# Forgetting attention's value projection, written tile by tile between the first thirteen slots with TensorE's order pinned

## The chip, the cores and the metric

One core of one Trainium2 chip runs the whole program. The metric is the device time of one execution, in microseconds (us). Engines are called PE (TensorE's matmuls), PEld (its weight loads), DVE (VectorE), ACT (ScalarE), POOL (GpSimd) and SP (SyncE, which here issues the transfers). Line numbers (L188) are those of the kernel before, where nothing else is said.

## The reference, cut to what matters

The reference is one decoder layer on 1024 tokens of width 1024. The first block has two groups of heads side by side on the same normalized input: four mLSTM heads of width 128 and eight heads of forgetting attention of width 64. A cross-attention and an MLP follow.

```python
h = rmsnorm(x, ln1[l])
z = h @ w_in[l]
ml_qk, ml_v, ml_o, ml_i, ml_f, fx_q, fx_k, fx_v, fx_f = jnp.split(z, splits, axis=-1)
...
mh = mlstm_chunkwise(mq, mk, mv, ig, lf)
...
fv = fx_v.reshape(B, S, FX_HEADS, FX_DH)
flf = jax.nn.log_sigmoid(fx_f.astype(jnp.float32) + fx_b_f[l].astype(jnp.float32))
fx_out = forgetting_attention(fq, fk, fv, flf).reshape(B, S, FX_W)
x = x + jnp.concatenate([ml_out, fx_out], axis=-1) @ w_out[l]
```

In `forgetting_attention` the scores of a block of 128 queries get a decay per key, are masked, go through a softmax, and weigh the values `fv`. The change is about where `fx_v`, a product of `h` (1024 x 1024) with 512 columns of weights, is computed in time.

## The kernel before

Every float32 operand of a large product is kept as a pair, high and low part (`split`, L131 to L138: ACT copies the high part, DVE forms the remainder), and a product is three matmuls (`mm3`, L183 to L188). The normalized input `h` lies in SBUF as pairs, features on partitions.

The order of the work is set in two ways. The program is traced in the order in which it is written, and a scheduler, which simulates the engines, then puts each engine's instructions in an order of its own: an instruction that is written later may stand earlier if it is ready earlier in that simulation. Where the code says `with in_order(...)` (L144), the instructions written inside are chained: on each named engine they keep their written order, behind the last instruction that was chained on it. Once built, each engine's order is fixed, and an engine waits at an instruction until its operands and its buffer are there.

Around the change stand these pieces:

- `ml_head(hd, ...)` (L568) is one mLSTM head, a generator in four steps. The first step goes over two halves of the tokens and four blocks of 128 keys in each: a score on PE into a bank of PSUM called "sc"; a decay on ACT (L586) with a mask on POOL (L588); their product on DVE (L589); its split on ACT and DVE (L134, L135); a sum over blocks on POOL (L593); and the product with the values on PE into the bank "ov". Sums over the 128 partitions (L217), a reciprocal root (L198 to L208, the power on POOL in L204) and the factors `fac` (L617) end the step. The next step turns the factors into a row (`to_row`: a transpose on PE in L249, a copy on ACT in L250, a transfer to DRAM in L251 and back to all partitions in L253). The third multiplies the first half's output with that row and the gate (L628, L629), splits and stores it, and loads the second half's row (L625). The fourth does the same for the second half. These three later steps are `closing`, and `next(closing, None)` runs one of them.
- "sc" has three banks that are used in turn, "tp" two, "mm", "m2" and "ov" one each. The last head's eight scores, its two groups of sums, the slots' scores and the row's transpose take the three "sc" banks in the order in which they are written.
- `slot(values, until)` (L1026) is a step of forgetting attention, one part of a score (up to 512 keys of 128 queries) after the other: the maximum of the part before on DVE (`top`, L741, L744), the exponential of the one before that on ACT (`exp`, L756), a scaling on POOL (L767), and the two matmuls of a new part's score (L734, L735). It is all under `in_order`. The first thirteen slots (`LEAD_`) run without values; from the fourteenth on, the probabilities are transposed (L782) and multiplied with the values (L801).
- `token_major(w_src, sink, cs, between)` (L488) is a projection with tokens on partitions. For each of two groups `c` of 256 columns it loads and splits two weight tiles (`weights`: "wr" has two buffers, "wh" and "wl" three each), and for each of eight blocks `t` of 128 tokens it runs 24 matmuls of 128x256 into a bank ("mm", "tp", "m2", "tp" in turn) and then `sink`. A tile in the text is one such block of 24 matmuls, numbered 0 to 15. Their three uses of "wh" and "wl" mean that group 1's second weight tile (k from 4 on) takes the buffer of group 0's first one, which is free when half of tile 7's matmuls are done.
- `fv_sink` (L649) splits the result (L137, L138) and stores it to DRAM (L652), from where a head's values are loaded later (L849).

Before, the thirteen slots are written first, then the projection as a whole. None of its instructions is under `in_order`, so the scheduler lays them wherever the engines have room.

## Time and profile before

| what | us |
|---|---|
| timed runs, median of 3 (lowest to highest) | 1511.64 (1510.98 to 1512.29) |
| span of the profiled execution | 1509.2 |
| timed median less that span (no other time of the profiled execution is given) | 2.4 |
| PE, sum of its busy time | 1493.0 |
| last mLSTM head's first key scores end, first value tile's matmul starts | 331.1 |
| slot 0's score on PE | 351.0 |
| first transpose of probabilities on PE (slot 13) | 392.8 |

A row of a timeline has the start in us, the length in us (of a group, where xN is over 1), the engine, the line, the operation, the tile written and those read, and, in brackets, how long the engine stood idle before it and what ended that. Matmuls overlap: one of 128x512 shows 0.39 us, but follows the one before after about 0.23 us. A row of busy times by stretches has the stretch, its length, each engine's busy time with the number of its instructions, the granted TensorE clock (1.00 is full speed), the share of the transfer engines and GB/s.

### The profile page before, as it was taken

The numbers are of one execution on the slowest core, as the hardware profiler recorded it, in microseconds if no ns is written. First come the engines' busy times: TensorE is split into PE (matmuls) and PEld (weight loads), VectorE is DVE, ScalarE is ACT, GpSimd is POOL, SyncE is SP. The second block draws the span as 40 slices with busy tenths as digits, with TensorE's granted clock in tenths as the row PEclk, the third lists the DMA queues.
The fourth block names the chain that finished last, engine by engine and source line by source line (L and its number), as shares of the span: only waits on it lengthen the run. The fifth ranks groups of instructions, "written<-read, shape, count | busy, mean of one in ns | idle before, by whom it ended". The sixth has DMA issues, their size and how long they took to land.

```text
span 1509.2 us, 22358 instructions
## 1 busy us (share of the span) xinstructions
PE 1493.0 (99%) x7806; PEld 1263.7 (84%) x7806; DVE 1122.7 (74%) x1803; ACT 757.7 (50%) x1440; POOL 528.7 (35%) x545
## 2 busy tenths in 40 slices
PE   9999999999999999999999999999999999999997
PEld 9988888889899888788988878888888888888887
DVE  7766676664788875667767899989996678787765
ACT  7324343334688764566654467566664521122134
POOL 1003030414365441623300044454544365553312
PEclk9999999999999999999999999999999999999999
DMA  6322333435777877853354447676678677776623
GB/s 243 115 79 95 98 108 126 132 129 153 247 261 256 284 248 246 271 169 126 128 182 159 147 155 279 235 261 248 217 273 292 264 279 279 279 272 251 247 88 112
DMA packets 124276, 303.04 MB, mean 201 GB/s; under 512 B 13810, under 2 KB 28460, under 8 KB 117252
## 3 DMA queue, kind: packets, MB, share of 16 engines
q1 hardware_dynamic: 124164, 301.62, 57.3%
q8 instruction: 61, 1.00, 0.3%
q14 instruction: 51, 0.42, 0.1%
HBM read 202.75 MB, written 98.82 MB: 200 GB/s over the span
## 4 chain that ended last, share of the span: by engine, by line
PE 90%; DMA 4%; DVE 3%; ACT 1%; issue 1%; POOL 1%; POOLq 0%; DVEq 0%; SPq 0%; ACTq 0%
PE tp L186 8%; PE tp L187 8%; PE tp L188 8%; PE sc L186 6%; PE sc L188 6%; PE sc L187 6%; PE mm L186 5%; PE m L188 5%; PE m L186 5%; PE m L187 5%; PE mm L188 5%; PE mm L187 5%; PE ov L801 2%; PE ov L186 2%; PE ov L187 2%; PE ov L188 2%
## 5 line engine op out<-in xcount | busy, mean ns | idle before, releaser
L186 PE MATMUL tp<-act,wl 128*128 128x512 f32 (+1 forms) x440 | 172.6, 392 | 0.0
L187 PE MATMUL tp<-act,wh 128*128 128x512 f32 (+1 forms) x440 | 172.1, 391 | 0.0
L188 PE MATMUL tp<-act,wh 128*128 128x512 f32 (+1 forms) x440 | 171.8, 392 | 0.0
L135 DVE TENSOR_TENSOR wl<-wr,wh 128x1024 fp32r<-128x1024 f32 (+2 forms) x99 | 131.4, 1327 | 27.0 <-ACT wh L134 26.7
L134 ACT ACTIVATE wh<-wr 128x1024 fp32r<-128x1024 f32 (+2 forms) x99 | 99.8, 1008 | 85.7 <-PE tp L188 32.7
L186 PE MATMUL mm<-act,wl 128*128 128x512 f32 (+1 forms) x332 | 124.8, 376 | 2.6 <-DVE r_c L138 2.1
L188 PE MATMUL mm<-act,wh 128*128 128x512 f32 (+1 forms) x332 | 124.1, 374 | 0.0
L187 PE MATMUL mm<-act,wh 128*128 128x512 f32 (+1 forms) x332 | 123.8, 373 | 0.0
L186 PE MATMUL m<-act,wl 128*128 128x512 f32 (+1 forms) x308 | 113.8, 369 | 0.6 <-DVE wl L135 0.6
L188 PE MATMUL m<-act,wh 128*128 128x512 f32 (+1 forms) x308 | 113.8, 369 | 0.0
L187 PE MATMUL m<-act,wh 128*128 128x512 f32 (+1 forms) x308 | 113.7, 369 | 0.0
L188 PE MATMUL sc<-act,wh 128*128 128x512 f32 (+1 forms) x280 | 105.6, 377 | 0.0
L187 PE MATMUL sc<-act,wh 128*128 128x512 f32 (+1 forms) x280 | 105.6, 377 | 0.0
L186 PE MATMUL sc<-act,wl 128*128 128x512 f32 (+1 forms) x280 | 105.6, 377 | 0.0
L1612 POOL TENSOR_TENSOR z<-wr 128x256 f32<-128x256 f32 x56 | 52.9, 966 | 131.8 <-DMA wr<-w_ff2q 126.7
L188 PEld LDWEIGHTS tp<-act,wh 128*128 128x128 f32 x440 | 82.7, 188 | 19.0
L186 PEld LDWEIGHTS tp<-act,wl 128*128 128x128 f32 x440 | 82.7, 188 | 18.5
L187 PEld LDWEIGHTS tp<-act,wh 128*128 128x128 f32 x440 | 82.7, 188 | 18.2
L134 ACT ACTIVATE wh<-z 128x1024 fp32r<-128x1024 f32 (+1 forms) x54 | 55.5, 1027 | 81.8 <-POOL z L1612 62.3
L135 DVE TENSOR_TENSOR wl<-z,wh 128x1024 fp32r<-128x1024 f32 (+1 forms) x54 | 77.7, 1439 | 11.4 <-ACT wh L134 11.4
L134 ACT ACTIVATE w<-wr 128x768 fp32r<-128x768 f32 (+3 forms) x35 | 28.0, 801 | 107.4 <-PE tp L186 33.0
L186 PEld LDWEIGHTS mm<-act,wl 128*128 128x128 f32 x332 | 62.7, 189 | 14.2 <-DVE r_c L138 2.6
(734 smaller groups left out, 4387.2 us busy)
## 6 DMA issues: line engine op xcount, KB each, us to landing
act<-right SPq DMA_DIRECT2D x49, 1024.0 KB
right<-w SPq DMA_DIRECT2D x56, 256.0 KB
wr<-w_ff2q SPq DMA_DIRECT2D x28, 512.0 KB
right<-r_d SPq DMA_DIRECT2D x49, 256.0 KB
right<-r_e SPq DMA_DIRECT2D x49, 256.0 KB
act<-fqk SPq DMA_DIRECT2D x48, 256.0 KB
wr<-w_in SPq DMA_DIRECT2D x20, 512.0 KB
wr<-w_ff SPq DMA_DIRECT2D x20, 512.0 KB
```

The source lines that it names most:

```text
L134: s.activation(hi, src, AF.Copy)
L135: return v.tensor_tensor(out=lo, in0=src, in1=hi.bitcast(F32), op=ALU.subtract)
L186: nc.tensor.matmul(ps, w[1], x[0], start=first, stop=False, skip_group_check=more)
L187: nc.tensor.matmul(ps, w[0], x[1], start=False, stop=False, skip_group_check=more)
L188: nc.tensor.matmul(ps, w[0], x[0], start=False, stop=last, skip_group_check=more)
L801: nc.tensor.matmul(self.ov[:, c0:], self.fv[:, self.j], t[:, c0:], start=self.j == 0 and t is self.p[1], stop=self.last and t is self.p[0])
L1612: g.tensor_tensor(out=o, in0=x, in1=y, op=op)
```

## The change

`token_major` yields after every tile, and its caller drives it. The projection's sixteen tiles are now written between the slots: two behind each of slots 0, 1 and 2 and one behind each of slots 3 to 12, and on PE (on PE alone) they are chained with the slots' matmuls. The steps of `closing` are now all written inside the loop: behind slots 1, 6 and 11, where before they stood behind slots 1 and 11 and ahead of the projection's tile 4.

```diff
                 sink(t, c, ps)
+                yield
...
-    token_major(a["w_mv"], mv_sink, (1,), {2: row_first, 4: gate_rows})
+    for _ in token_major(a["w_mv"], mv_sink, (1,), {2: row_first, 4: gate_rows}):
+        pass
...
+    fv_tiles = token_major(a["w_fv"], fv_sink)
     for i in range(LEAD_):
         slot(False, 0)
-        if i in (1, 11):
+        if i in (1, 6, 11):
             next(closing, None)
-    token_major(a["w_fv"], fv_sink, between={4: lambda: next(closing, None)})
+        with in_order((mybir.EngineType.PE,)):
+            for _ in range(1 if 2 < i else 2):
+                next(fv_tiles)
+    for _ in fv_tiles:
+        pass
```

What this does to the engines' orders, at three places. First PE, inside the last mLSTM head, where its first half's third score (`sc_3029`) ends. In rows of an order, the tile written stands ahead of the arrow; `tp_3367` and `mm_3338` are tiles of the values, `sc_` the head's scores, `ov_2997` its product with its values, `sc_3065` its sums. Before:

```order
L188 MATMUL sc_3029<-act_2587 128x256
L186 MATMUL tp_3367<-wh_3328,act_103 128x256
L187 MATMUL tp_3367<-wl_3329,act_102 128x256
L188 MATMUL tp_3367<-wh_3328,act_102 128x256
L186 MATMUL tp_3367<-wh_3328,act_103 128x256
```

Now, in the same place:

```order
L188 MATMUL sc_3029<-act_2587 128x256
L186 MATMUL sc_3045<-act_2587 128x256
L187 MATMUL sc_3045<-act_2587 128x256
L188 MATMUL sc_3045<-act_2587 128x256
L186 MATMUL ov_2997<-r_d_3006,act_107 128x512
L217 MATMUL sc_3065<-ones,r_b_2998 128x1
L186 MATMUL sc_3079<-act_2587 128x512
```

The values' matmuls are gone from here: 110 of them stood between this row and slot 0's score, and now none does. The first one follows slot 0's score (`sc_3207`), which needs the bank of the head's second to last score (`sc_3111`):

```order
L188 MATMUL sc_3127<-act_2587 128x256
L217 MATMUL sc_3146<-ones,r_b_2928 128x1
L186 MATMUL ov_3078<-r_d_3103,act_107 128x384
L736 MATMUL sc_3207<-act_3176 128x256
L737 MATMUL sc_3207<-act_3176 128x256
L186 MATMUL mm_3222<-wh_3212,act_103 128x256
```

(L736 and L737 of the changed kernel are L734 and L735 before.)

Second PE, at the transpose of the head's factors, `sc_3217` before and `sc_3287` now, with slot 2's score behind it (`sc_3226`, `sc_3354`). Before:

```order
L188 MATMUL tp_3618<-wh_3585,act_102 128x256
L249 MATMUL sc_3217<-ident,c_fac_2992 8x128
L734 MATMUL sc_3226<-act_3176 128x384
L735 MATMUL sc_3226<-act_3176 128x384
L734 MATMUL sc_3235<-act_3176 128x512
```

Now:

```order
L188 MATMUL tp_3321<-wh_3218,act_102 128x256
L249 MATMUL sc_3287<-ident,c_fac_2992 8x128
L736 MATMUL sc_3354<-act_3176 128x384
L737 MATMUL sc_3354<-act_3176 128x384
L186 MATMUL mm_3357<-wh_3212,act_105 128x256
```

Before, most of tile 9 (`tp_3618`) and parts of tiles 7, 8 and 10 stood ahead of the transpose; now it is tile 3 (`tp_3321`), and tile 4 (`mm_3357`) stands behind slot 2.

Third DVE, where the head's output is multiplied with the factors' row: `r_f_3062` is the first half, `r_f_2927` the second, `r_a` the row, `wl_` the remainder of the last weights. Before:

```order
L628 SCALAR_TENSOR_TENSOR r_f_3062<-r_f_3062,vec,r_a_3216 128x512
L138 SCALAR_TENSOR_TENSOR r_p_3672<-m_574_3647,rcol,r_p_3672 128x4x64
L629 SCALAR_TENSOR_TENSOR r_f_3062<-w_444_2931,r_f_3062 128x512
L741 TENSOR_REDUCE c_mx_3259<-sc_3261 128x1
L138 SCALAR_TENSOR_TENSOR r_c_3701<-tp_3676,rcol,r_c_3701 128x4x64
L138 SCALAR_TENSOR_TENSOR r_f_3062<-r_f_3062,r_y_3306 128x512
L628 SCALAR_TENSOR_TENSOR r_f_2927<-r_f_2927,vec,r_a_3311 128x512
```

Now (L629 and L630 are L628 and L629 before):

```order
L629 SCALAR_TENSOR_TENSOR r_f_2927<-r_f_2927,vec,r_a_3556 128x512
L630 SCALAR_TENSOR_TENSOR r_f_2927<-w_444_2931,r_f_2927 128x512
L746 ISA sc_3421,c_mx_3419<-sc_3421,causal 128x512
L746 ISA c_mx_3419 128x1
L766 RECIPROCAL c_den_3282<-c_den_3282 128x1
L138 SCALAR_TENSOR_TENSOR r_c_3411<-tp_3386,rcol,r_c_3411 128x4x64
L138 SCALAR_TENSOR_TENSOR r_f_2927<-r_f_2927,r_y_3745 128x512
L743 TENSOR_REDUCE c_mx_3458<-sc_3460 128x1
L766 RECIPROCAL c_den_3353<-c_den_3353 128x1
L138 SCALAR_TENSOR_TENSOR r_b_3449<-m_535_3424,rcol,r_b_3449 128x4x64
L135 TENSOR_TENSOR wl_3508<-wr_3505,wh_3507 128x1024
```

Before, the first half's normalization stood ahead of slot 6's maximum (`sc_3261`) and the second half's behind it, and the last weights were split far ahead of it. Now it stands ahead of slot 3's maximum (`sc_3421`) and slot 4's (`sc_3460`), and the remainder of the last weights (`wl_3508`) comes behind all of these.

## The prediction

> **What bounds the kernel now.** I read the page first, then the busy time by stretches around the place of the change, then the timelines of the engines there. The page's first part:

> ```profile
> span 1509.2 us, 22358 instructions
> PE 1493.0 (99%) x7806; PEld 1263.7 (84%) x7806; DVE 1122.7 (74%) x1803; ACT 757.7 (50%) x1440; POOL 528.7 (35%) x545
> ```

> TensorE (PE) sets the time: all its holes together are 1509.2 - 1493.0 = 16.2 us. So the change can win only holes, and every hole that it opens is paid in full, unless it closes another. The busy times by stretches (us, and in brackets the number of instructions):

> ```profile
> core 0: us, PE busy (x) PEld busy (x) DVE busy (x) ACT busy (x) POOL busy (x), PEclk, DMA share, GB/s
> 331.00:351.00 20.00, 20.00 (x162) 19.58 (x161) 11.80 (x21) 10.66 (x21) 8.09 (x11) 1.00 0.30 94
> 351.00:372.00 21.00, 21.00 (x176) 20.87 (x176) 9.50 (x26) 7.44 (x18) 8.61 (x8) 1.00 0.63 181
> 372.00:393.00 21.00, 19.59 (x154) 18.75 (x153) 13.51 (x40) 10.04 (x29) 5.80 (x10) 1.00 0.80 265
> 393.00:400.00 7.00, 6.01 (x40) 4.96 (x39) 5.79 (x20) 5.90 (x18) 2.58 (x7) 1.00 1.04 362
> 400.00:450.00 50.00, 50.00 (x375) 47.66 (x374) 42.28 (x117) 42.13 (x115) 30.87 (x43) 1.00 0.67 227
> ```

> From 331 to 372 us, where the last mLSTM head and the first two slots run, PE has no hole at all, though DVE, ACT and POOL are half idle: their steps wait for each other. Between 372 and 393 us PE has 1.4 us of holes, and these are the only ones in the values' projection; after 400 us it is full again, so what is lost here is not won back. From TensorE's row "L782 tp_3830" on (392.80 us before), every engine's order is the same in both kernels. The prediction is therefore the shift of that one row.

> **Part 1: the last head loses its filler.** Before, the projection's tiles stand between the head's steps. Now no tile may stand ahead of slot 0's score, which sits behind the head's second to last score (its bank of "sc" is that one's). TensorE before:

> ```profile
> 331.11 0.28 PE L186 MATMUL tp<-wh,act 128*128 128x256 f32 x1
> ...
> 342.23 0.28 PE L186 MATMUL m<-wh,act 128*128 128x256 f32 x1
> ...
> 343.88 0.28 PE L188 MATMUL m<-wh,act 128*128 128x256 f32 x1
> ...
> 350.99 0.28 PE L734 MATMUL sc<-act 128*128 128x256 f32 x1
> ```

> The tiles' matmuls follow each other every 1.65/14 = 0.118 us (from 342.23 to 343.88 us are 14 steps), so a tile of 24 is 2.83 us. From 331.11 us to slot 0's score the order of before holds 110 of them (tiles 0 to 3 whole, 14 of tile 4): 110 x 0.118 = 13.0 us that leave this stretch and come later. What comes back is only what they had delayed. Where the head waited for PE, and where it did not:

> ```profile
> 339.63 0.67 DVE L135 TENSOR_TENSOR r_e<-r_c,r_d 128x256 fp32r<-128x256 f32 x1 [0.21 <-ACT r_d L134]
> 341.64 0.28 PE L187 MATMUL ov<-r_e,act 128*128 128x256 f32 x1
> 342.07 0.60 ACT L603 ACTIVATE r_f<-ov 128x512 f32<-128x512 f32 x1 [0.41 <-PE ov L188]
> 342.57 0.59 ACT L604 ACTIVATE r_c<-ov 128x512 f32<-128x512 f32 x1
> 346.75 0.15 DVE L609 COPY c_sqs<-sc 128x4 f32<-128x4 f32 x1
> 347.47 0.89 DVE L589 SCALAR_TENSOR_TENSOR r_c<-sc,r_c 128x384 f32<-128x384 f32 x2 [0.57 <-POOL r_c L588]
> ```

> First, the half's last product had its operand at 340.30 us and ran at 341.64: 1.3 us late behind tiles, and ACT waited for it. Second, L589 freed slot 0's bank at 348.36 us and the score ran at 350.99: 2.6 us of queue, of which 0.7 us stays (a score, a sum and a product of the head, which now stand between). Between these two the links are ACT, POOL and DVE steps, which no tile touches; I give 0.1 us for them. Slot 0's score comes 1.3 + 1.9 + 0.1 = 3.3 us sooner, at 347.7 us. The matmul of the head that now stands ahead of it is 0.2 us. Term 1: 13.0 - 3.3 - 0.2 = 9.5 us lost, as holes between 331 and 348 us. Ends: 8 (if the middle links close up by 1.5 us too) and 11 us (if only the first delay goes).

> **Part 2: the factors.** Between tile 3 and slot 2's score now stands the transpose of the head's factors, which waits for this:

> ```profile
> 361.73 0.95 PE L217 MATMUL sc<-ones,r_c 128*128 128x1 f32 x8
> ...
> 364.08 0.17 DVE L198 TENSOR_SCALAR c_var<-c_sqs 128x8 f32<-128x8 f32 x1
> 364.33 1.65 POOL L204 TENSOR_TENSOR c_y<-c_var,half 128x8 f32<-128x8 f32 x1 [7.40 <-DVE c_var L198]
> 365.33 1.23 DVE L135 TENSOR_TENSOR wl<-wr,wh 128x1024 fp32r<-128x1024 f32 x1 [1.08 <-ACT wh L134]
> 366.87 1.18 DVE L206 TENSOR_TENSOR c_t<-c_y 128x8 f32<-128x8 f32 x1
> 368.96 0.17 DVE L617 TENSOR_TENSOR c_fac<-c_fac,c_rd 128x8 f32<-128x8 f32 x1
> 370.87 0.27 PE L249 MATMUL sc<-ident,c_fac 128*8 128x128 f32 x1
> ```

> Before, 6.45 us pass from the sums' end (362.68) to the factors (369.13), but some of that is DVE's other work (weights' remainders and an eviction), which the new order puts elsewhere: 1.6 us to the variance's end, 1.7 us on POOL and four DVE steps of 0.2 us are about 4.0 us. In the new order 14 matmuls of tile 3, 1.65 us, are all that is left behind the sums. Term 2: 4.0 - 1.65 = 2.3 us of hole, where nine tiles stood before. Ends: 0.5 (if the sums come earlier, between other rows) and 4.8 us (if the 6.45 stays).

> **Part 3: tile 8's weights behind the head's normalization.** The step of `closing` that stood behind slot 11 is now behind slot 6, and the one of tile 4 behind slot 11; the new order puts both halves of the normalization on DVE ahead of slot 3's maximum. Both wait for a row that goes out to DRAM and comes back. DVE is in order, so slot 3's and slot 4's maxima stand behind the second, ACT's exponentials behind these, and the split of the last weights (ACT, then DVE) behind those, although it is ready once tile 7 is half done. Tile 8 needs these weights for its second half. The rows: an earlier head's transpose and its second wait, this head's second wait, ACT's split (DVE's stands above, at 365.33), and PE's waits now:

> ```profile
> 310.98 0.28 PE L249 MATMUL sc<-ident,c_fac 128*8 128x128 f32 x1
> 319.84 0.75 DVE L628 SCALAR_TENSOR_TENSOR r_f<-r_f,vec,r_a 128x512 f32<-128x512 f32 x1 [0.63 <-DMA r_a<-facd]
> ...
> 383.57 0.75 DVE L628 SCALAR_TENSOR_TENSOR r_f<-r_f,vec,r_a 128x512 f32<-128x512 f32 x1 [1.52 <-DMA r_a<-facd]
> 364.24 1.06 ACT L134 ACTIVATE wh<-wr 128x1024 fp32r<-128x1024 f32 x1 [0.98 <-PE m L188]
> 381.98 0.44 PE L734 MATMUL sc<-act 128*128 128x384 f32 x1 [0.35 <-ACT act L756]
> ...
> 385.44 0.50 PE L734 MATMUL sc<-act 128*128 128x512 f32 x1 [1.07 <-ACT act L756]
> ```

> From the transpose to the second wait's end it took 319.84 - 310.98 = 8.9 us there, 383.57 - 370.87 = 12.7 us here. By part 1 slot 0's score is at 347.7; 82 tile matmuls and about 1.8 us of the head's lie ahead of the sums, so these end at 359.8, the factors are there at 363.8, and the second row lands at 363.8 + 8.9 to 12.7, say 374.0. From there DVE and ACT still have 1.4 us of normalization, a maximum, two evictions and another maximum (about 2.6 us), an exponential (0.7), and the split (1.06 + 1.23): 381.0 us. PE meanwhile does slot 2's score, tiles 4 to 7, three scores and half of tile 8: 364.0 + 4.5 x 2.83 + 1.6 = 378.3 us. Term 3: 381.0 - 378.3 = 2.7 us of hole; ends 1.4 (the row as fast as there) and 5.2 us (as slow as here).

> **Part 4: what is won.** The two holes of PE at slots 9 and 10 (0.35 and 1.07 us), where a score waits for an exponential, go: each slot now has one tile and a score, 2.83 + 0.24 to 0.47 us on PE, against some 2 us of DVE and less of ACT. Term 4: -1.4 us; ends -1.4 and 0. The evictions and stores of the tiles are the same in number, and cost nothing: they are spread over slots in which DVE and ACT have room, and the first reader of the values on PE is as far behind tile 15 as before. The change of SyncE's order costs nothing either: the second stack's loads now come ahead of the stores and are used only in slot 12; the 2 MB of memory tokens start later, after tile 10's store, some 18 us ahead of their first use.

> Sum: 9.5 + 2.3 + 2.7 - 1.4 = 13.1 us. The profiled span is 2.4 us below the median of the timed runs, and what lies around it stays: 1511.6 + 13.1 = **1524.7 us**. All low ends together give +8.5, all high ends +21; they do not all fall together, so the range is 1518.0 to 1530.5 (+6.4 to +18.9), which also takes in the rivals below but the last two.

> **A rule weighed.** What the trace shows of the clock when PE falls idle, at the program's end:

> ```profile
> 1500.00:1505.00 5.00, 1.06 (x8) 0.78 (x7) 2.85 (x8) 0.01 (x1) 0.71 (x1) 0.76 0.27 91
> 1505.00:1509.20 4.20, 0.00 (x0) 0.00 (x0) 0.27 (x1) 0.00 (x0) 0.00 (x0) 0.50 0.59 204
> ```

> The granted clock is 0.76 over five us with 1.06 us of work, and 0.50 with none; in all stretches above it is 1.00. The new longest hole is that ahead of the head's seventh score: squares ready at 341.9 (343.16 less the 1.3 us), eight sums until 342.8 (0.95 us, as in part 2's row), then nothing until L609's copy, now at 345.5: 2.7 us. [...]

> **Rivals.**
> - *The clock falls* in the thin stretch from 342.8 us on. Then the head's steps and tile 0's first 14 matmuls run at 0.50, as in the last row: 1.6 us of the head's matmuls ahead of slot 0 and 1.65 us of the tile's are doubled, +3.3 us: 1528.0. For it: PE is busy for some 7 of 16.6 us there. Against it: no hole as long as those of the end rows. Chance 0.12.
> - *Only part 1 counts*: the factors' and the weights' waits are hidden, since the scheduler's row order has slack that I don't see, or rows land early. 9.5 - 1.4 = +8.1: 1519.7. For it: the ends of terms 2 and 3 are small; against it, the order has no other row in these places. Chance 0.13.
> - *Not slower*: without tiles in front of them, the head's steps close up by all of the 13.0 us, and the 1.4 us of holes go: 1510.2. It decides at slot 0's score, which must then stand at 351.0 - 13.0 - 0.2, about 338 us. Against it: the first half's last remainder is formed on DVE at 339.63 us after a wait for ACT, not PE, and the whole second half is still to come. Chance 0.02; with something between, within 0.2%, another 0.02.
> - That the change doesn't do what it says can't be: the rows of the order show the tiles behind the slots.

> **How the numbers follow.** The forecast has 0.71. About 0.2% (3 us) is what a measurement of this kernel can tell from no change. Slower by more than that are the forecast and the first two rivals, 0.96; within it the not-slower rival's 1510.2 and what lies between, 0.03; faster by more 0.01, since all holes that go are 1.4 us.

> **What would show it.** Right: PE busy about 10 us of the stretch from 331 to 348 us, with waits of the head's scores and products for DVE and ACT; slot 0's score near 347.7 us, with tile 0 behind it; a wait of L249 for the factors of some 2 us near 364; a wait of tile 8 for the split weights near 380; the transposes of slot 13 near 406 instead of 392.8 us; all later stretches as before, moved by 13 us; clock 1.00 throughout. Wrong: slot 0's score before 345 us, no waits at 364 and 380 us, or a lower clock.

## The result and the profile after

The kernel after takes 1524.26 us (median of five runs, 1522.99 to 1529.44), the kernel before 1511.64: a ratio of 1.0087, 95% interval 1.0075 to 1.01. The profiled execution is the slowest of the five (1529.44 us); a second profile of the same kernel (e_again, below) has a span 2.5 us shorter, and where the two differ both numbers are given.

The page of the kernel after, its span and the busy sums:

```profile
span 1527.7 us, 22368 instructions
PE 1502.8 (98%) x7806; PEld 1270.2 (83%) x7806; DVE 1119.1 (73%) x1803; ACT 758.8 (50%) x1440; POOL 527.8 (35%) x545
```

PE runs the same 7806 matmuls as before, and yet it is busy 1502.8 - 1493.0 = 9.8 us longer. Its holes are 1527.7 - 1502.8 = 24.9 us, 8.7 more than the 16.2 of before. So only about half of the 18.5 us by which this execution's span is longer is waiting; the other half is matmuls that take longer (in e_again, the second profile, 7.9 and 8.1 us). The busy times by stretches show where (the column before the last two is the granted clock):

```profile
core 0: us, PE busy (x) PEld busy (x) DVE busy (x) ACT busy (x) POOL busy (x), PEclk, DMA share, GB/s
331.00:337.00 6.00, 2.00 (x11) 1.29 (x9) 4.33 (x7) 2.92 (x5) 0.00 (x0) 0.97 0.25 92
337.00:343.00 6.00, 6.00 (x19) 5.36 (x20) 2.65 (x6) 1.65 (x4) 3.04 (x4) 0.50 0.37 124
343.00:349.00 6.00, 4.71 (x20) 3.91 (x18) 1.62 (x2) 2.89 (x6) 1.83 (x3) 0.50 0.02 7
349.00:355.00 6.00, 5.66 (x28) 5.46 (x29) 3.42 (x8) 2.42 (x6) 5.39 (x6) 0.61 0.36 122
355.00:361.00 6.00, 6.00 (x52) 6.00 (x51) 2.11 (x7) 1.83 (x5) 3.59 (x5) 1.00 0.54 189
...
367.00:373.00 6.00, 3.83 (x24) 3.63 (x23) 1.79 (x8) 1.42 (x4) 2.01 (x2) 0.81 0.33 75
373.00:379.00 6.00, 6.00 (x47) 5.91 (x47) 2.78 (x5) 1.58 (x3) 0.00 (x0) 0.90 0.44 134
```

From 337 to 343 us PE is busy all the time, but with 19 matmuls, where 52 fill 6 us at a clock of 1.00 (355 to 361 us). Most of the 19 are wider than the tiles' 128x256, and all are slower: one of 128x512 follows the one before after 0.43 us here (338.36 to 338.79) and after 0.23 us at a clock of 1.00 (327.72 to 327.95). In stretches of 0.8 us, taken from 331.0 to 357.4 and from 364.0 to 380.0 us, the clock is 1.00 or 0.50 but for the four in which it changes. So the means of the stretches of 6 us give the time at half clock: 2 x 6 x (0.03 + 0.50 + 0.50 + 0.39) = 17.0 us in the last head, and 2 x 6 x (0.19 + 0.10) = 3.5 us more behind a second hole. PE's timeline has the rows that answer to those of the prediction:

```profile
335.31 0.39 PE L186 MATMUL sc<-act 128*128 128x256 f32 x1 [3.51 <-DVE r_b L590]
...
339.21 0.63 PE L188 MATMUL ov<-r_d,act 128*128 128x512 f32 x1
...
345.73 1.86 PE L217 MATMUL sc<-ones,r_c 128*128 128x1 f32 x8 [1.17 <-ACT r_c L605]
...
351.75 0.41 PE L736 MATMUL sc<-act 128*128 128x256 f32 x1
...
369.49 0.27 PE L249 MATMUL sc<-ident,c_fac 128*8 128x128 f32 x1 [2.17 <-DVE c_fac L618]
...
385.84 0.39 PE L187 MATMUL mm<-wl,act 128*128 128x256 f32 x1 [0.31 <-DVE wl L135]
...
409.60 0.60 PE L784 MATMUL tp<-ident,w 128*128 128x128 f32 x4
```

Slot 0's score stands at 351.75 us (before at 350.99, although 13.0 us of tiles now come behind it), L249 waits 2.17 us for the factors, and slot 13's transposes stand at 409.60 instead of 392.80. The longest hole is the first, 3.51 us: the head's fourth score needs a bank that DVE empties in L590. DVE came late to that, as its timeline shows:

```profile
331.98 0.69 DVE L642 SCALAR_TENSOR_TENSOR r_p<-mm,row 128x512 f32<-128x512 f32 x1 [2.93 <-DMA fqk<-r_p]
...
384.56 1.23 DVE L135 TENSOR_TENSOR wl<-wr,wh 128x1024 fp32r<-128x1024 f32 x1 [1.41 <-ACT wh L134]
```

The first row waits for the store of the keys to DRAM, whose buffer it writes next. The second is the remainder of the last weights: ready at 385.8 us, 0.3 us after PE wanted it.

### The profile page after: what moved, and what is told of

Its sections match the earlier page's. It is cut to its first block, busy times and chain, and to the rows that moved or that the text cites. A ratio compares the mean times of both kernels' runs of the same rounds, so it can differ in the third digit from the quotient of the medians.

```text
span 1527.7 us, 22368 instructions
## 1 busy us (share of the span) xinstructions
PE 1502.8 (98%) x7806; PEld 1270.2 (83%) x7806; DVE 1119.1 (73%) x1803; ACT 758.8 (50%) x1440; POOL 527.8 (35%) x545
## 4 chain that ended last, share of the span: by engine, by line
PE 66%; DMA 4%; DVE 3%; ACT 1%; issue 1%; POOL 1%; SPq 0%; POOLq 0%; DVEq 0%; ACTq 0%
PE sc L186 6%; PE sc L187 6%; PE sc L188 6%; PE tp L186 5%; PE tp L187 5%; PE tp L188 5%; PE m L186 4%; PE m L188 4%; PE m L187 4%; PE mm L186 4%; PE mm L187 4%; PE mm L188 4%; PE ov L803 2%; PE tp L784 2%; PE ov L186 2%; PE ov L188 2%
## 5 line engine op out<-in xcount | busy, mean ns | idle before, releaser
L186 PE MATMUL tp<-act,wl 128*128 128x512 f32 (+1 forms) x440 | 172.7, 392 | 0.0
L187 PE MATMUL tp<-act,wh 128*128 128x512 f32 (+1 forms) x440 | 172.1, 391 | 0.0
L188 PE MATMUL tp<-act,wh 128*128 128x512 f32 (+1 forms) x440 | 171.8, 391 | 0.0
L135 DVE TENSOR_TENSOR wl<-wr,wh 128x1024 fp32r<-128x1024 f32 (+2 forms) x99 | 132.1, 1334 | 28.7 <-ACT wh L134 28.4
L134 ACT ACTIVATE wh<-wr 128x1024 fp32r<-128x1024 f32 (+2 forms) x99 | 99.8, 1008 | 85.2 <-PE tp L188 32.8
L186 PE MATMUL mm<-act,wl 128*128 128x512 f32 (+1 forms) x332 | 124.6, 375 | 2.8 <-DVE r_c L138 2.4
L188 PE MATMUL mm<-act,wh 128*128 128x512 f32 (+1 forms) x332 | 123.8, 373 | 0.0
L187 PE MATMUL mm<-act,wh 128*128 128x512 f32 (+1 forms) x332 | 123.8, 373 | 0.0
L186 PE MATMUL m<-act,wl 128*128 128x512 f32 (+1 forms) x308 | 113.9, 370 | 1.0 <-DVE wl L135 0.8
L188 PE MATMUL m<-act,wh 128*128 128x512 f32 (+1 forms) x308 | 113.8, 369 | 0.0
L187 PE MATMUL m<-act,wh 128*128 128x512 f32 (+1 forms) x308 | 113.6, 369 | 0.0
L186 PE MATMUL sc<-act,wl 128*128 128x512 f32 (+1 forms) x280 | 105.7, 377 | 0.0
L188 PE MATMUL sc<-act,wh 128*128 128x512 f32 (+1 forms) x280 | 105.6, 377 | 0.0
L187 PE MATMUL sc<-act,wh 128*128 128x512 f32 (+1 forms) x280 | 105.6, 377 | 0.0
L188 PEld LDWEIGHTS tp<-act,wh 128*128 128x128 f32 x440 | 82.7, 188 | 19.0
L186 PEld LDWEIGHTS tp<-act,wl 128*128 128x128 f32 x440 | 82.7, 188 | 18.7 <-DVE r_f L1535 0.3
L187 PEld LDWEIGHTS tp<-act,wh 128*128 128x128 f32 x440 | 82.7, 188 | 18.2
L134 ACT ACTIVATE wh<-z 128x1024 fp32r<-128x1024 f32 (+1 forms) x54 | 55.5, 1027 | 82.0 <-POOL z L1619 62.5
L135 DVE TENSOR_TENSOR wl<-z,wh 128x1024 fp32r<-128x1024 f32 (+1 forms) x54 | 79.5, 1473 | 11.2 <-ACT wh L134 11.2
L134 ACT ACTIVATE w<-wr 128x768 fp32r<-128x768 f32 (+3 forms) x35 | 28.0, 801 | 106.8 <-PE tp L186 32.6
L186 PEld LDWEIGHTS mm<-act,wl 128*128 128x128 f32 x332 | 62.5, 188 | 14.5 <-DVE r_c L138 2.8
```

Of the source, the lines that this page charges most:

```text
L134: s.activation(hi, src, AF.Copy)
L135: return v.tensor_tensor(out=lo, in0=src, in1=hi.bitcast(F32), op=ALU.subtract)
L186: nc.tensor.matmul(ps, w[1], x[0], start=first, stop=False, skip_group_check=more)
L187: nc.tensor.matmul(ps, w[0], x[1], start=False, stop=False, skip_group_check=more)
L188: nc.tensor.matmul(ps, w[0], x[0], start=False, stop=last, skip_group_check=more)
```

## The experiments

Two theories stood after this profile. The first: the last head's own steps on ACT, POOL and DVE set when the factors are there, whatever PE does beside them; tiles that stand ahead of that point are free, and tiles that don't are paid in full. The second: PE's clock falls in the thin stretch, and the fall is the larger part of the loss.

**e_again: the kernel after, once more.**

> The changed kernel as it is, a second time, for a second trace beside those that follow. Theory A (the last mLSTM head lost its filler: holes on PE there, and the TensorE clock falls to 0.50 in that thin stretch): 1522 to 1529 us, granted clock near 0.5 from about 337 to 354 us again, slot 0's score at 350 to 352 us, slot 13's first transpose at 404 to 410 us. Theory B (the clock's fall was a chance of the one profiled execution, the loss is holes alone): clock 1.00 from 331 to 365 us, slot 0's score at 347 to 348 us, 1523 to 1525 us.

1526.06 us (1523.35 to 1528.29), ratio 1.0094 (1.008 to 1.0108). The second profile's busy times by stretches:

```profile
331.00:337.00 6.00, 3.68 (x15) 2.71 (x14) 5.23 (x9) 3.33 (x5) 0.39 (x1) 0.83 0.40 130
337.00:343.00 6.00, 5.59 (x22) 4.90 (x20) 1.40 (x3) 1.61 (x4) 2.65 (x4) 0.61 0.23 88
343.00:349.00 6.00, 4.14 (x17) 3.36 (x18) 3.23 (x6) 3.71 (x9) 3.29 (x5) 0.68 0.00 0
349.00:355.00 6.00, 6.00 (x40) 6.00 (x39) 2.24 (x5) 1.25 (x5) 5.82 (x6) 0.75 0.71 206
```

The fall repeats, though the first hole is 1.93 us here and not 3.51: 2 x 6 x (0.17 + 0.39 + 0.32 + 0.25) = 13.6 us at half clock. Slot 0's score stands at 349.78 (0.2 us ahead of the range expected), slot 13's transposes at 407.94 us. All nine runs of the kernel after together have a median of 1525.23 us, 13.6 above the kernel before. Each of the nine has a mean granted clock of 0.990 to 0.993, where 49 runs of the kernel before have 0.995 to 0.998, so the fall is no chance of the two profiles. But the two profiled executions are the slowest and the third slowest of the nine (1529.44 and 1526.88 us): in sum their stages lose more than a middle run does.

**e_no_pin: the tiles and the closing steps written as after, without the chain on PE.**

```diff
-        with in_order((mybir.EngineType.PE,)):
-            for _ in range(1 if 2 < i else 2):
-                next(fv_tiles)
+        for _ in range(1 if 2 < i else 2):
+            next(fv_tiles)
```

> The tiles are written between the slots as in the change, and the steps of closing too, but nothing of them is chained on PE. Theory A: the pin alone makes the loss, and the scheduler lays tiles 0 to 4 into the last head again: 1511.6 us, within 2 us of before, clock 1.00 from 331 to 392 us. Theory C (the places of the written tiles and of closing cost something by themselves): slower than 1515 us.

1511.64 us (1508.97 to 1513.45), ratio 0.9997 (0.9988 to 1.0006). Where the tiles are written doesn't matter as long as the scheduler may move them: it lays 10.4 tiles ahead of L249, as before. The chain alone makes the loss.

**e_two_ahead and e_five_ahead: two or five tiles written ahead of slot 0 and outside the chain, the rest as after.** The counts behind the slots become 2, 1, 1, ..., or 1 eleven times and then none.

```diff
-    for i in range(LEAD_):
+    for _ in range(2):
+        next(fv_tiles)
+    for i, n_ in zip(range(LEAD_), (2, 1, 1, 1, 1, 1, 1, 1, 1, 1, 1, 1, 1)):
...
-            for _ in range(1 if 2 < i else 2):
+            for _ in range(n_):
```

> As the change, but two tiles are written ahead of slot 0, unchained, and the other fourteen are chained, two behind slot 0 and one behind each later slot. Theory A: the first half of the last head is filled (no hole at 332 us), the second half is thin: 62 tile matmuls (7.3 us) are still missing there, less some 2 us that come back: 1516 to 1519 us; the clock falls later, after 343 us, or not at all. Theory B': the loss is made in the tight slots behind slot 0 (factors and last weights), so little changes: 1521 us or more.

> As the change, but five tiles are written ahead of slot 0, unchained, and eleven are chained, one behind each of slots 0 to 10. Theory A: PE's order in the last head is that of before, so its holes and the clock's fall go: slot 0's score near 352 us, clock 1.00 up to it; what stays is the wait for the factors (1.2 us: only one tile of 2.83 us stands against 4.0 us) and for the last weights (0 to 2.7 us): 1511 to 1515 us. Theory B' (tight slots make the loss): 1518 us or more.

Two ahead: 1524.52 us (1524.33 to 1525.97), ratio 1.0087 (1.0073 to 1.0101). The first expectation, 1516 to 1519, missed by over 5 us; the rival's, 1521 or more, fits. The two tiles filled the head's first half, where the clock now stays at 1.00, but the second half was as thin as ever:

```profile
343.00:349.00 6.00, 3.41 (x20) 2.64 (x19) 2.93 (x5) 3.78 (x8) 3.20 (x4) 0.86 0.37 103
349.00:355.00 6.00, 4.33 (x17) 3.52 (x17) 1.69 (x5) 1.61 (x5) 5.74 (x7) 0.50 0.76 252
```

The fall came there instead, and L249 waits 2.87 us at 369.29: what the two tiles gave early was lost again before the factors. Five ahead: 1513.9 us (1510.31 to 1515.74), ratio 1.0014 (1.0005 to 1.0023), as the first theory expected, and the rival's 1518 or more missed. Its stretches:

```profile
343.00:349.00 6.00, 6.00 (x53) 6.00 (x52) 2.69 (x5) 3.40 (x7) 2.15 (x4) 1.00 0.30 86
...
361.00:367.00 6.00, 4.31 (x24) 4.11 (x22) 2.27 (x12) 0.90 (x3) 1.65 (x1) 0.72 0.40 112
```

Both halves are full now, and the factors' transpose still stands at 367.07 us, where e_again has it at 367.63 with three tiles (8.5 us) fewer ahead of it. Those three tiles cost nothing there. What is left is L249's wait of 1.76 us (1.2 expected) and a fall of the clock, which can be seen in the times here: three runs with a mean clock of 0.998 took 1510.31 to 1513.59 us, six with 0.995 or 0.996 took 1513.9 to 1515.74. Among the nine runs of the kernel after no such order shows.

**e_seven_ahead and e_nine_spread: seven or nine tiles ahead of slot 0, the rest chained behind single slots.**

> Seven tiles ahead of slot 0 without an order of their own, nine pinned behind slots 0, 1, 2, 3, 4, 6, 8, 10 and 12. Five ahead gave 1513.9 with waits of 1.76 us at L249; nine may fill it all. By the filler theory seven lie between the two, nearer to the kernel before: 1511 to 1513, the wait at L249 under 1 us. Rival, the pin's own cost: as five, 1513 to 1515.

> Nine tiles are written ahead of slot 0 without an order of their own, so that the scheduler spreads them in the last head as before, and seven follow pinned behind slots 2, 3, 4, 6, 8, 10 and 12. If the loss of the kernel after is that the last head lost its filler, it is gone here: with what the pin can win (slots 9 and 10 wait 1.4 us in the kernel before) 1510.2 to 1511.8, and the clock 1.00 from 331 to 361. Rival, that the pin costs by itself, wherever it stands: 1513 to 1515, with waits at L249 or at the pinned tiles' weights.

1512.16 us (1510.27 to 1514.0), ratio 1.0005 (0.9996 to 1.0014); and 1511.47 us (1510.53 to 1514.01), ratio 1.0004 (0.9995 to 1.0012). Both equal the kernel before: the pin costs nothing by itself, and wins nothing. With nine tiles ahead of the factors the head's steps hardly move. Here are DVE's first product of the head and the first one of its second half, in e_nine_spread:

```profile
334.49 0.68 DVE L590 SCALAR_TENSOR_TENSOR r_b<-sc,r_b 128x512 f32<-128x512 f32 x1
...
345.75 0.69 DVE L590 SCALAR_TENSOR_TENSOR r_c<-sc,r_c 128x512 f32<-128x512 f32 x1 [2.04 <-POOL r_c L589]
```

and in e_again, with no tile beside it and the clock down:

```profile
333.25 0.68 DVE L590 SCALAR_TENSOR_TENSOR r_b<-sc,r_b 128x512 f32<-128x512 f32 x1
...
344.71 0.69 DVE L590 SCALAR_TENSOR_TENSOR r_c<-sc,r_c 128x512 f32<-128x512 f32 x1 [3.28 <-POOL r_c L589]
```

Between the two rows lie 11.26 and 11.46 us (11.32 in the kernel before, 12.12 in the kernel after's first profile); in e_warm and e_warm_pool (below), with no tiles and the clock at 1.00, it is 10.35 and 10.34 us (333.85 to 344.20, 333.10 to 343.44). DVE waits for POOL each time, POOL for ACT, and ACT for the product before. So tiles all around the chain lengthen it by 0.9 to 1.0 us, and their absence with the clock down by 1.1 to 1.8. That the clock alone makes the second difference is not shown: in e_warm and e_warm_pool PE also runs a product of the head ahead of the head's fifth score (at 336.03 and 336.79 us in e_warm_pool), where the kernel after has it behind (at 337.46 and 336.04 us in e_again).

**e_fill_factors: tile 4 behind slot 1, so ahead of L249.** Only the counts change, to 2, 3, 1, ..., 1.

> The kernel after with its counts 2, 3, 1, ... instead of 2, 2, 2, 1, ...: tile 4 stands behind slot 1 and so ahead of the factors' transpose L249, in place of behind slot 2. 24 matmuls of 128x256 are 2.8 us, as much as L249 waits (2.17 us). Waits only: that hole goes, the rest stays: 2.2 us less than the kernel after, 1521.5 to 1522.5, and the clock elsewhere as there. Waits and clock: the clock's second fall (0.72 and 0.89 for 6 to 16 us behind that hole) goes with it, another 1.3 to 2 us: 1520 to 1521. Rival: c_fac comes later by as much, since its chain is fed by TensorE's earlier work (the sums), or tile 4's own weights come too late: 1523 to 1525.

1525.32 us (1524.67 to 1525.76), ratio 1.0093 (1.0079 to 1.0106): nothing won, and 0.3 us above even the rival's range. The hole at L249 and the fall behind it are gone, and a new hole came at tile 8, in the timelines of PE and DVE:

```profile
381.90 0.39 PE L187 MATMUL mm<-wl,act 128*128 128x256 f32 x1 [1.88 <-DVE wl L135]
...
379.55 2.30 DVE L135 TENSOR_TENSOR wl<-wr,wh 128x1024 fp32r<-128x1024 f32 x1
```

PE comes there at 380.0 us, 5.5 sooner than in the kernel after (385.5), but the last weights don't come as much sooner (381.9 and 385.8 us). Two things hold them. Their split stands behind the head's normalization, as part 3 of the prediction says: the high part is ready at 377.99 us, and DVE comes to the remainder at 379.55. And the remainder takes 2.30 us here, where it takes 1.23 in the kernel after; POOL had 2.08 us of work from 379 to 385 us, and whether that is the reason was not tried. So 1.07 of the 1.88 us are the longer remainder and 0.8 the order.

**e_warm: matmuls that nobody reads, in the holes of the head's first half.** 33 of them, chained behind matmuls that stand there; `chain` is the same order-only dependency that `in_order` uses.

```diff
+    def warm(n, bank):
+        x = act_warm[0]
+        for _ in range(n):
+            early = next(i for i in reversed(nc.cur_bb.bb.instructions) if i.engine == mybir.EngineType.PE)
+            nc.tensor.matmul(bank, x[:, 0, :P], x[:, 0, : bank.shape[-1]], start=True, stop=True)
+            chain(nc.cur_bb.bb.instructions[-1], early)
...
+                if idle is not None and j == 2:
+                    before = warm(16, sp[:, :256])
...
+                if idle is not None and hf == 0 and d0 > 0:
+                    warm((0, 3, 2, 4)[d0], idle)
...
+            if idle is not None and hf == 0:
+                warm(8, idle)
```

> The kernel after, with 33 matmuls whose result nobody reads written into the last head's first half behind instructions that stand there: 16 of 128x256 behind its third score (in the unused columns of that score's bank), and 3, 2, 4 and 8 of 128x512 into a free bank behind the second, third and fourth products and the sums. They add no data that anything waits for; at full clock they are 16 x 0.118 + 17 x 0.235 = 5.9 us of TensorE work, in a stretch where TensorE was busy 7 to 8 of 17 us. Clock theory: the thin first half, not its holes alone, lets the clock fall, and the fall delays slot 0; filled, the clock is 0.95 or more from 331 to 361 us, slot 0's score stands at 347.5 to 349 (351.8 and 349.8 in the two profiles of the kernel after), slot 13's transposes at 404 to 406 (409.6 and 407.9), and the time is 1520 to 1523 though TensorE has more to do. Rival, holes only: the chain through VectorE and ScalarE sets slot 0's start and the clock's fall lies beside it, so that the added matmuls gain nothing: slot 0's score at 350 or later, 1524 to 1528. The wait at L249 (2.2 us) stays in both.

1527.88 us (1524.87 to 1530.96), ratio 1.011 (1.0094 to 1.0126): the clock theory's time missed. The stretches:

```profile
331.00:337.00 6.00, 4.03 (x27) 3.23 (x26) 5.05 (x9) 3.34 (x5) 0.12 (x1) 1.00 0.32 100
337.00:343.00 6.00, 5.99 (x32) 4.71 (x31) 3.16 (x5) 2.24 (x5) 3.02 (x4) 1.00 0.33 120
343.00:349.00 6.00, 5.43 (x29) 4.37 (x30) 3.09 (x5) 3.06 (x7) 4.20 (x5) 1.00 0.11 26
349.00:355.00 6.00, 3.82 (x19) 3.50 (x19) 1.12 (x4) 1.38 (x4) 5.80 (x7) 0.75 0.71 242
```

The clock did stay at 1.00 until 349 us, but slot 0's score still came at 351.55, behind a hole of 2.18 us. POOL's timeline has the reason:

```profile
347.02 3.65 POOL L728 MEMSET act<- 32x2048 f32 x2
350.74 0.29 POOL L615 TENSOR_SCALAR_AFFINE_SELECT r_c<-r_c 128x128 f32<-128x128 f32 x1
```

The added matmuls had changed the scheduler's order elsewhere: two memsets of 1.8 us now stood ahead of the selection that slot 0's bank waits for. The kernel tells nothing of the clock's price.

**e_warm_pool: the same, with POOL's memsets and the last sums held where the kernel after has them.**

```diff
+            if stacks:
+                chain(nc.cur_bb.bb.instructions[-1], selects[6])
...
+            if i == 1:
+                third = [z for z in nc.cur_bb.bb.instructions[at_:] if z.engine == mybir.EngineType.PE and "atmul" in type(z).__name__]
+                chain(third[10], sums[-1])
```

> e_warm again, with GpSimd's 32x2048 memsets of the second stack held behind the head's seventh selection (in e_warm they had moved ahead of it and slot 0's score waited 2.2 us for that), and the last sums held ahead of tile 3's eleventh matmul, as they stand in the kernel after. If the clock's fall in the last head costs time: clock 0.95 or more from 331 to 367 us, slot 0's score at 348.0 to 349.5, L249's transpose at 365 to 366.5 (369.5 and 367.6 in the two profiles of the kernel after), slot 13's transposes at 404.5 to 406.5, 1520 to 1523. If the head's steps on ScalarE, GpSimd and VectorE set slot 0 and the factors by themselves: L249 at 367 or later, 1524 to 1527, whatever the clock.

1523.85 us (1523.48 to 1525.97), ratio 1.0086 (1.0071 to 1.0101). Stretches and PE's timeline:

```profile
331.00:337.00 6.00, 5.10 (x32) 4.18 (x31) 5.30 (x9) 3.48 (x6) 0.87 (x1) 1.00 0.40 137
337.00:343.00 6.00, 5.75 (x34) 4.59 (x32) 2.42 (x4) 2.86 (x6) 2.27 (x4) 1.00 0.21 81
343.00:349.00 6.00, 5.83 (x36) 4.96 (x37) 4.13 (x9) 2.96 (x8) 4.46 (x6) 1.00 0.24 74
349.00:355.00 6.00, 6.00 (x53) 6.00 (x52) 0.57 (x2) 1.24 (x5) 5.66 (x6) 1.00 0.72 238
...
361.00:367.00 6.00, 3.85 (x30) 3.65 (x30) 3.22 (x15) 1.10 (x5) 1.65 (x1) 0.95 0.37 109
367.00:373.00 6.00, 6.00 (x42) 6.00 (x42) 2.10 (x4) 1.73 (x4) 0.38 (x1) 0.77 0.20 69
```

```profile
347.70 0.28 PE L774 MATMUL sc<-act 128*128 128x256 f32 x1
...
365.64 0.27 PE L249 MATMUL sc<-ident,c_fac 128*8 128x128 f32 x1 [2.15 <-DVE c_fac L654]
...
405.32 0.60 PE L822 MATMUL tp<-ident,w 128*128 128x128 f32 x4
```

With the clock held, slot 0's score stands at 347.70 us, L249 at 365.64 and slot 13's transposes at 405.32, as the clock theory has them (slot 0 is 0.3 us sooner), though PE has 5.9 us more to do. The time lies between the two theories' ranges. Counted from DVE's first L590 of the head, so that the first hole's length drops out, L249 stands at 32.5 us here (first row at 333.10), at 34.4 in e_again and at 34.9 in the kernel after. So the fall ahead of the factors costs 1.8 to 2.4 us in those two executions, if the other order of PE's product and fifth score costs nothing. The times of the runs don't separate it: 1523.85 against 1525.23 us, with ranges that overlap.

**e_warm_all: 16 more such matmuls ahead of L249, for the second fall.** To stand there, the first step of `closing` is written ahead of slot 2, behind tile 3, and no longer ahead of tile 2.

```diff
+        if i == 2:
+            before = warm(16, last_sp[0][:, 256:], sums[-1])
+            at_ = len(nc.cur_bb.bb.instructions)
+            next(closing, None)
...
-        if i in (1, 6, 11):
...
+        if i in (6, 11):
             next(closing, None)
```

> e_warm_pool, and 16 more of the 128x256 matmuls that nobody reads (1.9 us at full clock) between tile 3 and the factors' transpose L249, in the 2.2 us that it waits, so that no hole of TensorE over 1.5 us is left from 331 to 409 us. If the clock falls behind holes of that size, it is now 1.00 from 331 to 409 us, and what the second fall cost (clock 0.81 and 0.90 from 367 to 379 us: 6 x 0.19 + 6 x 0.10 = 1.7 us) is won against e_warm_pool: slot 13's transposes 1.5 to 2 us sooner than there, 1518.5 to 1521.5. If the clock's falls cost nothing because other engines set the end: the time of e_warm_pool, within 1 us, or up to 1 us later for the added work.

1527.17 us (1525.45 to 1528.59), ratio 1.0101 (1.0084 to 1.0118): missed by both theories. PE's waits in the stretch:

```profile
PE sc L249 <- DVE c_fac L657: 1.0, 1, 1.0
PE mm L187 <- DVE wl L135: 0.9, 1, 0.9
PE sc L186 <- DVE r_b L623: 0.8, 1, 0.8
PE mm L186 <- ACT wh L134: 0.7, 1, 0.7
```

The clock was 1.00 from 331 to 379 us, as meant, and PE reached the place where tile 8 waits 14.5 us behind L249, where it took 16.0 us in both profiles of the kernel after. But the last weights were ready 16.4 us behind L249 (383.78 us), as in all of these kernels but e_warm: 16.3 in the kernel after, 16.6 in e_again, 16.0 in e_warm_pool. So what the clock gave, PE waited for them, 0.9 + 0.7 us. Two things changed on the way to that and nearly cancel: the factors' row came later (from the end of ACT's copy in L250 to DVE's first multiplication with the row it took 6.1 us, 368.00 to 374.11, and 4.4 in e_warm_pool, 366.22 to 370.57), and ACT and DVE had taken an eviction and a normalization in another order, which was 1.4 us shorter (first multiplication with the row to ready weights, 9.7 us, and 11.0 in e_warm_pool). The clock then fell behind the waits (0.93 and 0.78 from 379 to 391 us), and slot 13's transposes came at 409.15.

What the second fall costs by itself stays unsettled. In the kernel after it takes up most of the time that PE would else have waited for the last weights (16.0 against 14.5 us, with the weights at 16.3 and 16.6). From L249 to slot 13's transposes it is 40.1 and 40.3 us in the two profiles of the kernel after, and 39.0 in e_warm, which has the same order on PE there and a clock of 1.00 throughout (369.74 to 408.76 us). Of these 1.1 to 1.3 us a part is not the clock's: the last weights are ready 15.2 us behind L249 there.

**What they say together.** The tiles ahead of the factors' transpose are counted in the built programs, the times are PE's:

| kernel | tiles ahead of L249 | L249, us | slot 13's transposes, us | between, us |
|---|---|---|---|---|
| before | 10.4 | 370.87 | 392.80 | 21.9 |
| e_nine_spread | 9 | 370.81 | 394.92 | 24.1 |
| e_seven_ahead | 9 | 369.68 | 393.70 | 24.0 |
| e_five_ahead | 7 | 367.07 | 396.59 | 29.5 |
| e_two_ahead | 5 | 369.29 | 407.69 | 38.4 |
| e_fill_factors | 5 | 368.34 | 405.55 | 37.2 |
| after, e_again | 4 | 369.49, 367.63 | 409.60, 407.94 | 40.1, 40.3 |
| e_warm_pool | 4 | 365.64 | 405.32 | 39.7 |

L249 stays within 5.2 us, whether 4 or 10.4 tiles (18.1 us of matmuls apart) are ahead of it. What isn't ahead of it stands behind it and is paid there: 40.1 - 21.9 = 18.2 us, less the 1.4 to 3.2 us by which L249 came sooner. With the clock held it comes 5.2 us sooner and no more. Up to seven tiles the head's chain covers for nothing as the kernel stands (L249 is no later than with four, and 1.4 us later than with four and the clock held); with nine the whole loss is gone.

## Why the prediction was right, and where it wasn't

- **Sign and size.** Forecast +13.1 us, measured +12.6 by the medians of five runs and +13.6 with all nine of the kernel after. PE is the bound, and the holes of the last head are not won back. The end of the program moves as slot 13's transposes do, to within 1.7 us in every kernel above.
- **Part 1, the last head loses its filler.** The mechanism was right, and the size only under a condition that failed. Slot 0's score was forecast at 347.7 us; it stands at 351.75 and 349.78 in the kernel after, and at 347.70 in e_warm_pool, where the clock is held. Counted from the head's first L590, it stands at 18.1 us in the kernel before and at 14.6 in e_warm_pool: 3.5 us sooner, 3.3 by the forecast. By the prediction's own sum term 1 was 13.0 - 1.2 - 0.2 = 11.6 us in e_again and 13.0 + 0.8 - 0.2 = 13.6 in the first profile, not 9.5, both above its upper end of 11. The reason given, that tiles delay the chain in a few places and that its other links are ACT, POOL and DVE steps that no tile touches, fits the chain's lengths: up to the second half the tiles add 1.0 us (11.3 against 10.3), where I had put their first delay at 1.3.
- **The clock: the step that failed.** I said that the longest new hole would be 2.7 us, ahead of the head's seventh score, and that the clock would stay at 1.00; that a hole of that length leaves the clock alone was not shown by any row of before. The longest hole was ahead of the fourth score (3.51 and 1.93 us), where DVE waits for a store that I had not followed: with the tiles gone PE has nothing between the third and the fourth score. And the longest hole's length was the wrong test, since the clock fell in e_again too, where the longest ahead of it was 1.93 us, and again behind L249's 2.17 us. So the rival *The clock falls* happened. It asked 3.3 us for the fall; 1.8 to 2.4 us stand against that in the two profiles (from e_warm_pool, with its condition).
- **Part 2, the factors.** 2.3 us forecast, 2.17 measured in both profiles. The place was off: near 364 us forecast, 365.64 with the clock held, 367.63 and 369.49 without.
- **Part 3, the last weights.** 2.7 us forecast, 0.3 and 0.6 measured, and the mechanism was right. The weights were forecast 17.0 us behind L249 (381.0 and 364.0 us) and came 16.3 and 16.6 us behind it. PE was forecast there 14.3 us behind L249, and so it was with the clock at 1.00 (14.6 in e_warm, 14.5 in e_warm_all). In the kernel after it took 16.0 us: the second fall, 3.5 us at half clock and so about 1.7 us of work, filled most of the wait. So the fall and the wait are not to be added.
- **Part 4, what is won.** Right: no score of the slots waits for an exponential between slot 0 and slot 13's transposes in the kernel after.
- **The sum.** In the two profiles slot 13's transposes came 16.8 and 15.1 us later than before, 13.1 by the forecast. The factors, forecast at 364.0 us, were 5.5 and 3.6 us late, and from there to the transposes it took 40.1 and 40.3 us, 41.9 by the forecast. So two errors cancel in part, the clock that was not to fall and the weights' wait that its second fall filled. That the median time came within 1 us of the forecast is luck besides: these two executions are among the slowest of the nine, and no middle one was profiled. Of the first profile's 18.5 us, 8.7 are holes and 9.8 longer matmuls; I had all of it as holes.

## What to carry to other kernels

Work without deadlines is worth most beside a chain that PE can't speed up. Before pinning it elsewhere, find the point at which that chain ends (here the factors' transpose) and count the work that stands ahead of it. Compare PE's busy sum as well as its holes: here, with the same instructions, a longer busy sum was a lower clock (9.8 us longer at a mean granted clock of 0.990, where the kernel before has 0.997), and it grew by as much as the holes. That isn't yet time: part of it lay under a wait that would have come anyway. And if a filled hole gains nothing, look for the next operand that was late under its cover.

## What the runs showed of the hardware

The length of a hole doesn't decide alone. L249's wait of 2.17, 2.17 and 2.15 us was followed by a fall in the kernel after, e_again and e_warm_pool (in e_two_ahead the clock fell within a wait of 2.87 us: L249's matmul takes 0.38 us there, and 0.27 in the others), and one of 2.16 us at the same instruction was not in e_warm; neither were e_fill_factors' 1.88 us at tile 8 and e_five_ahead's 1.76 us at L249. In e_five_ahead the clock fell ahead of that, at 361.3 us, behind two holes of 0.29 and 0.47 us with eight sums of one column behind them. Nor does work bring the clock back at once: in the kernel after PE's rows have no hole from 336.91 to 344.55 us, 7.6 us and so more than two such lengths, and the clock stayed at 0.50 until about 353.7. What brings a fall, and what ends it, these runs don't settle. The same program also fell by different amounts in its two profiles, 20.5 us at half clock and 17.0.
